# Small products of a hybrid decoder step on one Trainium2 core: samples' turns joined, transpositions and updates in one visit

## The chip, the core and the metric

The kernel runs on one core of one Trainium2 chip. TensorE does matrix products and transpositions into PSUM, VectorE and ScalarE do elementwise work and bring results out of PSUM, GpSimd does a little elementwise work and issues some stores, and SyncE issues most DMAs. The metric is the device time of one execution in microseconds. Before the change it is 835.4 us, the median of 3 runs (835.07 to 835.62).

## What is computed

One inference step of one decoder layer, for a prompt of 1024 tokens and 32 sample tokens (8 sequences of 4), model width 1024. After a conditioned RMSNorm, one wide projection feeds two branches, an mLSTM matrix memory with 4 heads in chunks of 128 tokens and a sliding-window attention with sinks (8 heads of 64, 2 key heads). Their outputs are gated, merged and projected back:

```python
h, gate = adaln_in(x, c, w_ada, b_ada, g_norm)
(mq, mk, mv, mi, mf, mo, mz, aq, ak, av, az, gm, ga) = split_in(h @ w_in)
y_m, C, n, m = mlstm_branch(mq, mk, mv, mi, mf, mo, mz, C0, n0, m0, b_i, b_f, g_mn)
...
o = sink_attend(...)
y_a = o.astype(x.dtype) * jax.nn.silu(az)
u = jax.nn.sigmoid(gm) * (y_m @ w_mo) + jax.nn.sigmoid(ga) * (y_a @ w_ao)
x = x + gate * (u @ w_o)
```

A final RMSNorm gives y. The new matrix memories, normalisers and stabilisers of prompt and samples, and the new key and value caches, are outputs too. Everything is float32.

## The kernel before

**Wide products.** A float32 product is made of three products of a faster float32 format: each operand is split into a high and a low part (hi, lo), and hi*hi, hi*lo and lo*hi are summed in PSUM. The first part of the projection runs one block of 128 columns at a time (job, job_part). From the key job of the first mLSTM head on, the columns of the projection are taken two blocks at a time, as Pair objects, and each pair is multiplied by a seven-product scheme over 2 x 2 blocks (block_products): products 1 to 7, each of 4 x 3 wide matmuls with 512 columns, into PSUM tiles bx, bw, by, bz. There are 18 pairs: four of head_in (queries, keys and values of the mLSTM heads), eight of gate, two of query_gate and four of head_gate. The order of the products is 5, 6, 2, 7, then product 1 of the next pair, then 3, 4 (for the first pair 6, 2, 7, 1 of the next, 5, 3, 4). Afterwards att_products does the same for the attention output in four AttPair objects (ax, aw, ay, az), then come mem_out and the rows of the output projection.

**The samples of a pair.** The seven-product scheme covers the 1024 prompt tokens alone. The 32 sample columns of a pair are multiplied in full float32 in Pair.samples(): 16 products with 32 output rows each (a column tile of the array), which the trace shows as 32 instructions smp (128*32). They leave four partial sums in four groups of 32 partitions of a "b" bank, which ScalarE copies to SBUF (smps). Pair.samples_end() adds the four groups by one product with a constant (smpo, two instructions in the trace, 128*128) into another "b" bank, and the kind of the pair takes the result from there. Before the change samples() of the next pair is called at the end of product 2 of a pair (product 7 for the first), and samples_end() at the end of the pair's own product 6. AttPair has the same two functions; its small products are smpa (128*32) and smpo.

**Visits.** All other work with small products (attention units, the chunks of an mLSTM head, the sample heads, the gates) is written as generators that run beside the wide products. Side.tick() is called after each k of a wide product and at the end of each product. A generator yields a lag and the names of the PSUM banks that its next step uses ("b", "o"), and tick() lets the step run when the lag is over on the kernel's own clock (side.now, line 258, an estimate in microseconds), when the banks have been left alone for HOLD (2.0 for "b", 4.0 for "o"), and, if it uses banks, when 1.5 have gone by since the last step with products (line 146). Two steps with the same bank are not run in one tick. The order of TensorE is the order of the program; VectorE and ScalarE are ordered by the framework in this stage. Each of the PSUM groups "g", "a", "b" and "o" has two banks.

**Generators that the change touches.** head(h) is one mLSTM head of the prompt: it loads, forms decays, transposes keys and values (tk, tv), and multiplies (S, U, n), in three groups of chunks (GROUPS, 3 + 3 + 2 chunks). At its end stage_c3(p) scales the rows of a group on VectorE, and stage_d(p) transposes them (ty), scales them on ScalarE and stores them. sample_head(h) does one head's samples: products stk, sS, sn, then the update of the 8 sequences' memories in three groups (sU), then the sum st and the transposition sty. The four sample heads run one after another. gates() works out the forget and input gates near the start. The "half" pool (ht) holds 49 tiles of 128 x 512 that nearly all of this work shares.

## Time and profile before

| | |
|---|---|
| median of 3 runs | 835.4 us (835.07 to 835.62) |
| the profiled execution, its own time | 835.73 us |
| its span in the profile | 833.9 us |
| TensorE busy | 813.9 us, 98% of the span |
| VectorE busy | 597.2 us, 72% |
| ScalarE busy | 421.7 us, 51% |
| mean DMA rate | 185 GB/s |
| granted TensorE clock | 0.999 |

The rows that follow in the prediction come from the profile's page, from the view of waits and from the timeline. A row of the timeline has the start (us from the span's start), the time from the first start to the last end, the engine, the line of the kernel, the operation, the tiles written and read, the array used (rows*columns), the shape of the moving operand, and the number of instructions merged into the row. The ends of matmuls overlap the starts of the next ones, so distances are taken between starts. A line can be that of a helper: L260 is mm, L265 is tr, L221 is any operation of VectorE or ScalarE. A row of waits has the waiting instruction, the one that released it, the sum, the number and the longest of the waits in us.

### The profile page before, as it was taken

What the parts mean: (1) busy time and instruction counts of PE and PEld (TensorE: products, weight loads), DVE (VectorE), ACT (ScalarE), POOL (GpSimd) and SP (SyncE); (2) the same over time, 40 slices, a digit from 0 to 9 for tenths busy, and PEclk for the clock granted to TensorE, in tenths of its full rate; (3) what the DMA queues carried; (4) which work ended last, traced back from release to release, by engine and by line L of the source; (5) the groups of instructions that cost most, each with busy time, mean ns of one, the idle gap of its engine ahead of it and who ended that gap; (6) DMA issues with size and microseconds to landing.
All of it is one profiled execution on the core that took longest, in us unless ns stands there. A gap on an engine that the chain in (4) does not pass through costs nothing. (4 is left out here: it accounts for less than half of the span.)

```text
span 833.9 us, 15075 instructions
## 1 busy us (share of the span) xinstructions
PE 813.9 (98%) x5129; PEld 665.7 (80%) x5129; DVE 597.2 (72%) x1501; ACT 421.7 (51%) x1032; POOL 67.0 (8%) x128
## 2 busy tenths in 40 slices
PE   6999999999999999999999999999999999999996
PEld 3779897888787788888888877778777779997775
DVE  4899886656656455666666776787878988874776
ACT  5664365655565564535464545344445654334343
POOL 0120000000000000000000100000002104250000
PEclk9999999999999999999999999999999999999999
DMA  9996756346445423589845433554346685643532
GB/s 342 387 362 216 197 191 203 118 155 212 140 136 162 113 102 107 172 258 309 267 146 191 134 132 113 167 178 128 128 153 205 200 287 185 205 139 127 202 108 107
DMA packets 106688, 153.95 MB, mean 185 GB/s; under 512 B 20448, under 2 KB 54368, under 8 KB 106580
## 3 DMA queue, kind: packets, MB, share of 16 engines
q1 hardware_dynamic: 100964, 142.25, 52.3%
q10 hardware_dynamic: 4176, 6.56, 2.1%
q0 software_dynamic: 1472, 4.20, 1.3%
q8 instruction: 40, 0.66, 0.3%
q14 instruction: 36, 0.29, 0.1%
HBM read 109.22 MB, written 44.75 MB: 185 GB/s over the span
## 5 line engine op out<-in xcount | busy, mean ns | idle before, releaser
L221 ACT ACTIVATE p<-p,nmx 128x256 f32<-128x256 f32 (+1 forms) x64 | 31.0, 485 | 15.6 <-DVE nmx L221 15.2
L260 PE MATMUL g_aq<-h_h,wh_aq 128*128 128x384 f32 (+1 forms) x96 | 32.3, 336 | 0.0
L221 DVE CUSTOM_DVE_ANT_0 p<-sc,cst,sink 128x256 f32<-128x256 f32 (+1 forms) x64 | 26.2, 463 | 8.3 <-PE sc L260 8.2
L260 PE MATMUL g_aq<-h_h,wl_aq 128*128 128x384 f32 (+1 forms) x96 | 30.9, 322 | 0.0
L260 PE MATMUL g_aq<-h_l,wh_aq 128*128 128x384 f32 (+1 forms) x96 | 30.8, 321 | 0.0
L260 PE MATMUL g_w_mo<-ym_l,wh_w_mo 128*128 128x384 f32 (+1 forms) x96 | 30.8, 321 | 0.0
L260 PE MATMUL g_w_mo<-ym_h,wh_w_mo 128*128 128x384 f32 (+1 forms) x96 | 30.8, 321 | 0.0
L260 PE MATMUL g_w_mo<-ym_l,wl_w_mo 128*128 128x384 f32 (+1 forms) x96 | 30.8, 321 | 0.0
L248 POOL DMA_DIRECT2D oD<-uqv x16 | 8.9, 554 | 200.0 <-ACT uqv L221 162.8
L221 ACT ACTIVATE et<-et,an 128x128 f32<-128x128 f32 x32 | 11.2, 395 | 20.7 <-DVE et L221 19.2
L260 PEld LDWEIGHTS g_aq<-h_h,wh_aq 128*128 128x128 f32 x96 | 18.0, 188 | 2.6 <-issue 1.5
L260 PE MATMUL sc<-ukv,uqv 64*128 64x256 f32 (+1 forms) x128 | 18.3, 390 | 1.3 <-DVE p L221 1.2
L221 DVE COPY p<-pt 128x512 f32<-128x512 f32 (+1 forms) x16 | 10.5, 655 | 12.0 <-PE pt L265 12.0
L260 PEld LDWEIGHTS g_w_mo<-ym_l,wh_w_mo 128*128 128x128 f32 x96 | 18.0, 188 | 0.0
L260 PEld LDWEIGHTS g_aq<-h_l,wh_aq 128*128 128x128 f32 x96 | 18.0, 188 | 0.0
L260 PEld LDWEIGHTS g_w_mo<-ym_h,wh_w_mo 128*128 128x128 f32 x96 | 18.0, 188 | 0.0
L260 PEld LDWEIGHTS g_w_mo<-ym_l,wl_w_mo 128*128 128x128 f32 x96 | 18.0, 188 | 0.0
L260 PEld LDWEIGHTS g_aq<-h_h,wl_aq 128*128 128x128 f32 x96 | 18.0, 188 | 0.0
L221 ACT ACTIVATE p<-p,den 128x256 f32<-128x256 f32 (+1 forms) x32 | 14.2, 490 | 7.4 <-DVE den L221 7.3
L221 ACT ACTIVATE sq<-rows_h 128x512 f32<-128x512 f32 (+2 forms) x14 | 8.2, 582 | 17.7 <-issue 12.0
L260 PE MATMUL g_mq<-h_h,wh_mq 128*128 128x384 f32 (+1 forms) x48 | 16.8, 350 | 0.3 <-ACT mk L221 0.3
L221 DVE TENSOR_TENSOR wor<-wor,gb 128x512 f32<-128x512 f32 x16 | 10.7, 689 | 8.7 <-DMA wor<-w_out 8.6
(2078 smaller groups left out, 2852.1 us busy)
## 6 DMA issues: line engine op xcount, KB each, us to landing
x<-xT SPq DMA_DIRECT2D x16, 256.0 KB, 5.1
early_h<-w_ada SPq DMA_DIRECT2D x8, 512.0 KB, 8.8
adar_ga<-w_ada SPq DMA_DIRECT2D x16, 256.0 KB, 4.2
wr_ga<-w SPq DMA_DIRECT2D x16, 256.0 KB, 3.4
wr_gm<-w SPq DMA_DIRECT2D x16, 256.0 KB, 3.3
taD<-gt SPq DMA_DIRECT2D x16, 256.0 KB, 2.0
tmD<-gt SPq DMA_DIRECT2D x16, 256.0 KB, 4.2
wor<-w_out SPq DMA_DIRECT2D x16, 256.0 KB, 5.3
```

Of the source, the lines that this page charges most:

```text
L221: ins = f(*args, **kw)
L248: ins = (eng or nc.sync).dma_start(out, in_)
L260: in_order(nc.tensor.matmul(out, lhsT, rhs, start=start, stop=stop, skip_group_check=more))
```

## The change

- block_products: samples_end() of a pair is no longer called behind its product 6, but directly before samples() of the next pair, behind product 2 (product 7 for the first pair). For the last pair it is called before product 3. Behind samples(), the "b" bank is marked as used and tick(True) offers a visit whether the quiet time is over or not; first_sums() comes after that visit.
- att_products: samples_end() likewise moves from behind product 6 to product 2, directly before samples() of the next pair; the last pair keeps its place.
- head(): the three scalings and the three transpositions become one step each. The third transposition goes to an "o" bank.
- sample_head(): the three updates sU run in one step, the third in an "o" bank. The scaled sum ns lies in the tile z instead of a tile of its own.
- gates(): four scratch tiles and nm, wi become parts of one tile of the "half" pool, taken at the start. The pool gets a 50th tile, and a spacer tile of 56 columns (LEAD) goes.

```diff
@@ -36,7 +36,6 @@
 
 C_ID, C_S9, C_TRI, C_CM, C_AM, C_TS, C_CS, C_RS, C_S32, C_BM, C_S64 = 0, 128, 137, 265, 393, 649, 681, 713, 745, 777, 785
 C_END = 849
-LEAD = 56
 
 
 def shape_constants():
@@ -138,12 +137,12 @@
                 if item in st["live"]:
                     st["live"].remove(item)
 
-    def tick(self):
+    def tick(self, visit=False):
         self.each()
         for st in self.streams.values():
             if st["wait"] and len(st["live"]) < st["max"] and self.now >= st["next"]:
                 self.begin(st)
-        used, visit = set(), self.now >= self.last + self.quiet
+        used, visit = set(), visit or self.now >= self.last + self.quiet
         for item in sorted((i for st in self.streams.values() for i in st["live"]), key=lambda i: i[1]):
             banks = set(item[2])
             if self.now < item[1] or used & banks or (banks and not visit) or any(self.now < self.free.get(b, 0) for b in banks):
@@ -193,7 +192,7 @@
             return ps.tile(shape, F32, tag="o", bufs=2, name=name)
 
         def ht(shape, name, dt=F32):
-            return sp.tile(shape, dt, tag="half", bufs=49, name=name)
+            return sp.tile(shape, dt, tag="half", bufs=50, name=name)
 
         def sm(shape, name, bufs=3, dt=F32):
             return sp.tile(shape, dt, tag=name, bufs=bufs, name=name)
@@ -306,7 +305,6 @@
         issue(small, a["small"])
         load_x(0, 2, KT, xT[0])
         load_x(1, 0, KT, xT[1])
-        cp.tile([128, LEAD], F32, name="lead")
         cst = cp.tile([128, C_END], F32, name="cst")
         vec = cp.tile([128, 28], F32, name="vec")
         cT, xS = (small[:, o:o + KT * n].rearrange("p (k n) -> p k n", k=KT) for o, n in ((C_TRI + 28, 9), (C_TRI + 28 + KT * 9, NS)))
@@ -598,18 +596,16 @@
         def gates(gp, zg, bias):
             gate_sums(gp, zg, (8,))
             ig = cp.tile([128, 36], F32, name="ig")
-            x = cp.tile([128, 36], F32, name="fx")
+            gt2 = ht([128, 512], "gt2")
+            x, e, r, q = (gt2[:, 256 + 36 * i:292 + 36 * i] for i in range(4))
             for t, o in ((ig, 0), (x, 4)):
                 V.memset(t, 0.0)
                 V.tensor_tensor(t[:, 0:32].rearrange("p (h c) -> p h c", c=8),
                                 gp[:, 0:8, o:o + 4].rearrange("p c h -> p h c"),
                                 bias[:, o:o + 4].unsqueeze(2).to_broadcast((128, 4, 8)), op=ALU.add)
                 V.tensor_tensor(t[:NS, 32:36], gp[:NS, 8, o:o + 4], bias[:NS, o:o + 4], op=ALU.add)
-            e = cp.tile([128, 36], F32, name="fe")
             S.activation(e, x, AF.Abs)
             S.activation(e, e, AF.Exp, scale=-1.0)
-            r = cp.tile([128, 36], F32, name="fr")
-            q = cp.tile([128, 36], F32, name="fq")
             lf = cp.tile([128, 36], F32, name="lf")
             V.tensor_scalar(r, e, 2.0, None, op0=ALU.add)
             V.reciprocal(r, r)
@@ -637,9 +633,8 @@
             tr(tp[:4, 2, 0:NS], an[:NS, 32:36], ident[:NS, :NS])
             mm(tp[:4, 3, 0:NS], lf[:NS, 32:36], cst[:NS, C_TS:C_TS + NS], start=True, stop=True)
             gt4 = ht([32, 4, 128], "gt4")
-            gt2 = ht([32, 2, 128], "gt2")
             aT, bT, zero, cm = (gt4[:, i] for i in range(4))
-            nm, wi = gt2[:, 0], gt2[:, 1]
+            nm, wi = gt2[:32, 0:128], gt2[:32, 128:256]
             aTs = cp.tile([NH, NS], F32, name="aTs")
             bTs = cp.tile([NH, NS], F32, name="bTs")
             V.tensor_copy(aT, tp[:32, 0])
@@ -1134,7 +1129,7 @@
                 m = len(cs)
                 c0, w = cs[0] * 128, m * 128
                 ns = w_.pop(p)
-                ty = pb([128, 3, 128], f"ty{h}_{p}")
+                ty = (pb, pb, po)[p]([128, 3, 128], f"ty{h}_{p}")
                 for i in range(m):
                     tr(ty[:, i], ns[:, i, 0:128], ident)
                 y = ht([128, 384], "yt")[:, :w]
@@ -1146,8 +1141,8 @@
                           [(stage_e, 1), (stage_c, 0), (stage_a, 1), 7.0, "o"],
                           [(stage_b, 1), (load, 2), 10.0, ""], [(prep, 2), 3.0, "ob"],
                           [(stage_e, 2), (stage_c, 1), (stage_a, 2), 7.0, "o"], [(stage_b, 2), 5.0, "o"],
-                          [(stage_c, 2), 5.0, ""], [(stage_f, 0), 4.0, ""], [(stage_c3, 0), 4.0, "b"],
-                          [(stage_d, 0), (stage_c3, 1), 4.0, "b"], [(stage_d, 1), (stage_c3, 2), 4.0, "b"], [(stage_d, 2), 0.0, ""]):
+                          [(stage_c, 2), 5.0, ""], [(stage_f, 0), 4.0, ""], [(stage_c3, 0), (stage_c3, 1), (stage_c3, 2), 6.0, "ob"],
+                          [(stage_d, 0), (stage_d, 1), (stage_d, 2), 0.0, ""]):
                 for fn, p in visit[:-2]:
                     fn(p)
                 yield visit[-2:]
@@ -1216,19 +1211,17 @@
             S.copy(ns4, num)
             for c, b, m in zip(Cs, bs, ns_):
                 V.tensor_tensor(c[:, :m], c[:, :m], sxb[:, h, 2, b].unsqueeze(2).to_broadcast((128, m, 129)), op=ALU.mult)
-            yield 4.0, "b"
+            yield 4.0, "ob"
             for i, (c, b, m) in enumerate(zip(Cs, bs, ns_)):
-                up = pb([128, 388], f"sU{h}_{i}")
+                up = (pb, pb, po)[i]([128, 388], f"sU{h}_{i}")
                 mm(up[:, :m * 129 + m % 2], kn, vms[i][1][:, :m * 129 + m % 2], start=True, stop=True)
                 V.tensor_tensor(c[:, :m], c[:, :m], up[:, :m * 129].rearrange("p (b e) -> p b e", e=129), op=ALU.add)
                 store(a["C_s"][h][:, b], c[:, :m, 0:128])
                 G.tensor_copy(at["n1"][:, h, b], c[:, :m, 128])
-                if i == 1:
-                    yield 1.5, "b"
             yield 3.0, "o"
             tot = po([128, 129], f"st{h}")
             mm(tot[:NS], cst[:, C_S32:C_S32 + NS], ns4, start=True, stop=True)
-            ns = sm([NS, 129], "sns", 1)
+            ns = z[:NS, 0:129]
             S.copy(ns, tot[:NS])
             ssq = sm([NS, 1], "sssq", 2)
             jk = sm([128, 128], "mjk", 2, BF16)
@@ -1524,6 +1517,8 @@
                 job_ = jobs[n]
                 nxt = jobs[n + 1] if n + 1 < len(jobs) else None
                 hook(n, i)
+                if i == 3 and not nxt:
+                    job_.samples_end()
                 job_.kind.ahead(job_, i)
                 if i == (5 if n else 6) and nxt:
                     nxt.load()
@@ -1545,7 +1540,6 @@
                         side.tick()
                 if i == 6:
                     Y = filled(pa, "by", W, n)
-                    job_.samples_end()
                 elif i == 2:
                     job_.done(0, 0, X)
                 elif i == 5:
@@ -1558,7 +1552,10 @@
                 if i == (7 if n else 5):
                     job_.done(1, 1, p5, Y)
                 if i == (2 if n else 7) and nxt:
+                    job_.samples_end()
                     nxt.samples()
+                    side.free["b"] = side.now + HOLD["b"]
+                    side.tick(True)
                     nxt.first_sums()
                 if j == 0 or (i == 3 and nxt):
                     X = NX
@@ -1742,10 +1739,12 @@
 
                 if i == 6:
                     Y = copy_of(pa, "ay", W)
-                    job_.samples_end()
+                    if not nxt:
+                        job_.samples_end()
                 elif i == 2:
                     job_.done(0, 0, X)
                     if nxt:
+                        job_.samples_end()
                         nxt.samples()
                         nxt.first_sums()
                 elif i == 5:
```

## The prediction

> **What bounds the kernel now.** I read the busy line of the page first, then TensorE's own waits, then the timeline of TensorE around the small products that the change moves.
>
> The busy line of the page:
>
> ```profile
> PE 813.9 (98%) x5129; PEld 665.7 (80%) x5129; DVE 597.2 (72%) x1501; ACT 421.7 (51%) x1032; POOL 67.0 (8%) x128
> ```
>
> Who kept TensorE waiting (us in total, times, longest):
>
> ```profile
> core 0 of [0], span 833.9 us
> ...
> PE sc L260 <- DVE p L221: 1.2, 1, 1.2
> PE bx L260 <- DVE zt L221: 0.8, 1, 0.8
> ...
> PE smpo L260 <- ACT hv L221: 0.3, 1, 0.3
> ...
> PE by L260 <- DVE hg1z L221: 0.2, 1, 0.2
> ```
>
> TensorE is busy for 98% of the span, and from the paired stage (block_products) on its waits are fractions of a microsecond to 1.2 us, none of them for a DMA. So the time of this kernel is the sum of the steps from one product's start to the next on TensorE, and an edit is worth what it takes from or adds to that chain of starts. The number of visits, work on VectorE and ScalarE, and transfers count only where one of them makes a product wait. All prices below are distances between starts. Durations are not used, because matmuls overlap.
>
> **Price of a small full-array burst.** First the timeline of TensorE around one smpo (two instructions, 128*128 array) with nothing joined to it:
>
> ```profile
> 548.20 0.33 PE L260 MATMUL smpo<-cst,smps 128*128 128x64 f32 x2
> 548.35 0.47 PE L260 MATMUL bx<-h_h,wh_pquery_gate__6438 128*128 128x512 f32 x1
> 548.66 0.40 PE L260 MATMUL bx<-h_l,wh_pquery_gate__6438 128*128 128x512 f32 x1
> 548.89 0.39 PE L260 MATMUL bx<-h_h,wl_pquery_gate__6439 128*128 128x512 f32 x1
> 549.12 0.39 PE L260 MATMUL bx<-h_h,wh_pquery_gate__6438 128*128 128x512 f32 x1
> ```
>
> A wide product (512 columns) follows the last after 0.23 us. From the burst's start to the second wide product behind it there are 548.66 - 548.20 = 0.46 us, where without the burst there would be one wide step of 0.23. The smpo burst costs 0.23 us. The first wide product behind it holds the array for 0.31 instead of 0.23, which looks like a fixed charge of 0.08 us per burst. Two bursts of transpositions show whether it is one:
>
> ```profile
> 335.00 0.49 PE L265 MATMUL ty<-cst,et 128*128 128x128 f32 x3
> 335.24 0.48 PE L260 MATMUL bx<-h_h,wh_pgate__3991 128*128 128x512 f32 x1
> 335.56 0.39 PE L260 MATMUL bx<-h_l,wh_pgate__3991 128*128 128x512 f32 x1
> ...
> 340.01 0.38 PE L265 MATMUL ty<-cst,et 128*128 128x128 f32 x2
> 340.14 0.48 PE L260 MATMUL by<-t3h,wh_pgate__4023 128*128 128x512 f32 x1
> 340.46 0.39 PE L260 MATMUL by<-t3l,wh_pgate__4023 128*128 128x512 f32 x1
> ```
>
> Three cost 0.56 - 0.23 = 0.33 us, two cost 0.45 - 0.23 = 0.22. That is 0.11 each and nothing per burst: the 0.08 behind a burst is the last product's own remainder, not a charge for changing over.
>
> **Price of a tiled burst.** The products of samples() use 32 columns of the array (128*32). One of their bursts, with the wide products around it:
>
> ```profile
> 250.48 0.40 PE L260 MATMUL bx<-h_h,wl_phead_in__3096 128*128 128x512 f32 x1
> 250.81 0.30 PE L260 MATMUL smp<-wr_mv,c 128*32 128x128 f32 x2
> ...
> 251.61 0.28 PE L260 MATMUL smp<-wr_mq,c 128*32 128x128 f32 x2
> 251.82 0.50 PE L260 MATMUL by<-t3h,wh_phead_in__3131 128*128 128x512 f32 x1
> 252.15 0.39 PE L260 MATMUL by<-t3l,wh_phead_in__3131 128*128 128x512 f32 x1
> ```
>
> Here the entry takes 0.33 (0.10 over a wide step), and the exit 0.21 with 0.33 behind it. The burst costs 1.67 - 0.46 = 1.21 us, for eight steps of four products side by side. So only a burst that leaves the full-array form has a charge at its ends, and a join can save only that.
>
> A rule of the Trainium skill goes further: the page TensorEngine Tiling (Array Packing), section Key Properties, says that changing the tiling mode, and not just the tile, drains TensorE. By that rule alone nothing is saved where full joins full, and nothing where smpo joins smp either, since the change of mode between them stays; the joins would then be worth 0 and the time would stay near 835. This page's drain agrees with the entry of 0.33 against 0.23, and the next row shows that the join is not quite worth 0.
>
> The trace has one smpo that stands directly ahead of a tiled burst (oT, 128*64, not 128*32):
>
> ```profile
> 273.25 0.39 PE L260 MATMUL bw<-t2h,wl_phead_in__3365 128*128 128x512 f32 x1
> 273.48 0.33 PE L260 MATMUL smpo<-cst,smps 128*128 128x64 f32 x2
> 273.74 0.44 PE L260 MATMUL oT<-p,ukv 128*64 128x128 f32 x4
> ```
>
> Joined, the tiled burst begins 0.23 + 0.26 = 0.49 us after the last wide product. Apart, smpo costs 0.23 and the tiled entry 0.33, together 0.56. **A join of smpo ahead of smp saves 0.07 us.** Bounds for the form that isn't shown (128*32 behind smpo): 0, if the drain is the same wherever it falls, to 0.23, if smpo vanished in it; I take 0.07, the nearest row.
>
> A visit behind the samples is shown too, here with 20 full-array products:
>
> ```profile
> 277.40 0.39 PE L260 MATMUL bx<-h_h,wl_phead_in__3408 128*128 128x512 f32 x1
> 277.72 0.30 PE L260 MATMUL smp<-wr_mk,c 128*32 128x128 f32 x2
> ...
> 280.98 0.48 PE L260 MATMUL by<-t3h,wh_phead_in__3433 128*128 128x512 f32 x1
> 281.29 0.39 PE L260 MATMUL by<-t3l,wh_phead_in__3433 128*128 128x512 f32 x1
> ```
>
> It costs 3.89 - 0.46 = 3.43; apart it would be 1.21 + 20 x 0.11 = 3.41. Such a join saves nothing.
>
> **The change, part by part.**
>
> Samples' turn: there are 18 pairs, so 17 turns in which smpo now stands ahead of smp. One of the smpo was joined to oT already and loses that. Net 16 x 0.07 = 1.1 us. The three turns of the attention pairs with a next pair (smpa, the same 128*32 form) give 0.2. The last pair's smpo moves to the step before product 3, where hook(n, i) has just issued smpa: it adds 0.15 and then 0.31 instead of 0.33 behind it, 0.13 instead of 0.23, saving 0.1. Together **-1.4**.
>
> The forced visit: samples() issues 32 products that the kernel's own clock (line 258) counts as 32 x 128/2400 = 1.7, more than the 1.5 of quiet, so the tick at the end of the same turn was already allowed to visit. Forcing it opens nothing. What is new is that visits using a "b" bank are barred there for 2.0. Full-array visits lose nothing by going alone (above). One visit to "b" behind a smp is tiled, a sample head's transposition sty:
>
> ```profile
> 506.30 0.39 PE L260 MATMUL bx<-h_h,wl_pgate__5956 128*128 128x512 f32 x1
> ...
> 507.63 0.24 PE L265 MATMUL sty<-cst,sns 32*128 32x32 f32 x1
> ```
>
> Alone it pays its own entry and exit: 0 more if it finds another tiled burst, up to 0.10 in and 0.10 out. I take **+0.2**.
>
> The forced visit also puts its VectorE work ahead of first_sums()' three additions. Between them and the first split of their result lie products 7 and 1, 24 wide steps, 5.5 us. That cover hides them; without it product 5 would wait as long as the visit's VectorE work takes.
>
> Transpositions of a head, three bursts to one, four heads: 8 bursts fewer at 0 each. Bounds 0 to 0.08 each (the remainder above), so 0 to 0.6; I take 0. The third ty takes an "o" bank, so three evacuations on ScalarE come together. Sample head's updates (sU), two bursts to one, four heads: no join of theirs is shown, bounds 0 to 0.08 each, so 0 to 0.3; I take 0, as for ty.
>
> Buffers: the "half" pool gets a 50th buffer, the gates' scratch moves into a tile of it that is held longer, samples' sums are held one product longer, ns moves into z over a column of vn whose last reader is two visits earlier. No instruction is added. The cover is that no wait of TensorE was for a load. If the pool ran dry, a load would start later and a split with it; that lies in the upper range. Addresses shift too: wide products keep the step of 0.23 in bx and by, whose operands lie in different tiles (rows above), so I price that at 0.
>
> Waits: the smpo wait of 0.3 is at a place that no longer has one, and VectorE's three small operations of the last smpo now stand behind hg1z instead of ahead of it, so the 0.2 there may go. **-0.5**. Each turn now takes both "b" banks at once. Where a visit shortly before has used them, smpo or smp waits for ScalarE's evacuation, as smpo did once for 0.3: bounds 0 to 17 times, I take one, **+0.3**. The sc and bx waits (1.2, 0.8) hang on where visits fall; they may go or have a sibling, taken at 0 with 2 us either way.
>
> Sum: -1.4 + 0.2 - 0.5 + 0.3 = -1.4 us. The profiled execution took 835.73 us (1.8 outside its span), 0.3 over the median of 835.4. From it 834.3, and against the median **834.0 us**.
>
> **Rivals.**
>
> (1) A burst does have a price: 0.08 for each that vanishes. Then the 8 ty, 4 sU and 20 smpo give 32 x 0.08 = 2.6 in place of 1.4, and if the sc wait goes as well (1.2) the time is 834.0 - 1.2 - 1.2 = 831.6, or 832.8 without it. For it: the longer wide product behind every burst. Against: two and three ty differ by exactly one product.
>
> (2) The joins are worth nothing, since the drain is paid wherever it falls: 834.0 + 1.4 = 835.4. For it: one sighting only, with another tile form. Against: that sighting.
>
> (3) Slower: both "b" banks in one turn. TensorE is in order, so a smpo that waits for its bank holds everything behind it, the next pair's products included; VectorE and ScalarE then get the pair's evacuations late. At 0.3 a turn five turns eat the gain; with 10 or more of 17 the kernel is slower by over 0.2%, and at 14 of them (13 more than the one in the sum, 3.9) it takes 837.9; I take 837.5. For it: the one smpo wait, of just this kind. Against: smp, which has its place already, does not stand among TensorE's waits for another engine, and visits to "b" are now held off behind it.
>
> **Chances.** Forecast 834.0: 0.43 (own range 833.0 to 835.2). Rival (1): 0.22. Rival (2): 0.12. Rival (3): 0.23. 0.2% (1.67 us) is about what a measurement can tell from no change. Faster by more means below 833.7: rival (1) and under half of the forecast, 0.41. Slower means above 837.1: two thirds of (3), 0.15, and 0.03 for moved waits in the other cases. The rest, 0.41, is within. The range takes rival (1) as far as its lower figure and a third of rival (3): 831.6 to 837.2, with 0.2 left out, most of it above.
>
> **What would show it.** In the changed kernel: smpo directly ahead of smp, with 0.26 between their starts and 0.33 behind (right) or over 0.30 between (rival 2). Eight ty in one burst that costs 0.88 (right) or 0.72 (rival 1). TensorE's waits: a smpo or smp wait on ScalarE in more than five turns is rival (3). I would be wrong most plainly if TensorE's total of waits moved by more than the joins did, in either direction.

## The result, and the profile after the change

The changed kernel takes 838.64 us (median of 5 runs, 837.92 to 840.19), the kernel before 835.4 us beside it. The ratio is 1.0043, with a 95% interval of 1.0031 to 1.0055. So it is slower by about 3.6 us (2.6 to 4.6 by the interval), outside the predicted range (831.6 to 837.2). Its profiled execution took 840.19 us.

The busy line and the granted clock in 40 slices, from the page of the changed kernel:

```profile
PE 815.0 (97%) x5129; PEld 670.2 (80%) x5129; DVE 595.7 (71%) x1501; ACT 420.5 (50%) x1032; POOL 69.8 (8%) x128
...
PEclk9999999999999999999899999999999999999998
```

TensorE's waits in the changed kernel (us in total, times, longest):

```profile
PE xc L259 <- ACT xsq L220: 6.2, 1, 6.2
PE S L259 <- DVE C L220: 5.9, 1, 5.9
PE pt L264 <- DVE mx L220: 1.2, 1, 1.2
...
```

The waits that the prediction quoted (sc 1.2, bx 0.8, smpo 0.3, by 0.2) are all gone by name. Where sc waited, at 287 us, pt now waits for VectorE as long (1.2), and one long wait is new: a product S of a head waits 5.9 us for VectorE's memory update C. And the twentieth slice of the clock (398 to 419 us) shows an 8.

**The joins do what they were priced at.** A joined turn of the samples and a head's joined transpositions, from the timeline of TensorE of the changed kernel:

```profile
490.99 0.39 PE L259 MATMUL bx<-h_h,wl_pgate__5730 128*128 128x512 f32 x1
491.21 0.33 PE L259 MATMUL smpo<-cst,smps 128*128 128x64 f32 x2
491.47 0.30 PE L259 MATMUL smp<-wr_ga,c 128*32 128x128 f32 x2
...
495.36 1.03 PE L264 MATMUL ty<-cst,et 128*128 128x128 f32 x8
496.15 0.48 PE L259 MATMUL bx<-h_h,wh_pgate__5800 128*128 128x512 f32 x1
496.46 0.40 PE L259 MATMUL bx<-h_l,wh_pgate__5800 128*128 128x512 f32 x1
```

smp follows smpo after 0.26, as oT did in the kernel before. Eight transpositions in one burst cost 496.46 - 495.36 - 0.23 = 0.87 us, which is 8 x 0.11 and nothing per burst.

**Where the time went.** I aligned the starts of the same wide products in two traces (by tile and count, from TensorE's first product). The table has "this kernel minus the kernel before" in us at times of the kernel before, counted from its first product, which starts 7.1 us into the span: 386 to 406 in the table is 393 to 413 in its timeline. Between 240 and 660 us the visits lie at other places, so small differences there come and go; a jump between two columns does not.

| kernel | 239 | 345 | 386 | 406 | 446 | 566 | end |
|---|---|---|---|---|---|---|---|
| changed | +1.1 | +0.7 | +2.0 | **+10.6** | +10.9 | +6.4 | +4.9 |

The front differs by 1.1 us; kernels whose front is that of the kernel before show 0.3 to 0.8 there, so most of it is the spread between executions. Between 386 and 406 us the changed kernel loses 8.6 us; over the rest of the paired stage it gains. The place in the timeline of TensorE of the changed kernel:

```profile
405.26 0.38 PE L264 MATMUL tv<-cst,hv 128*128 128x128 f32 x2
411.49 1.23 PE L259 MATMUL S<-hq,hk 128*128 128x128 f32 x4 [5.85 <-DVE C L220]
412.37 0.77 PE L259 MATMUL bw<-t2h,wh_pgate__4792 128*128 128x512 f32 x1
412.94 0.63 PE L259 MATMUL bw<-t2l,wh_pgate__4792 128*128 128x512 f32 x1
413.37 0.63 PE L259 MATMUL bw<-t2h,wl_pgate__4793 128*128 128x512 f32 x1
```

The burst (n, tk, tv and S) takes 8.67 us from its first start at 403.70 to the next wide product; without a wait it takes 2.14. That is 6.5 too many. Behind it the wide step is 0.43 instead of 0.23 for some ten steps, another 2.0. The row for 410 to 415 us below has a granted clock of 0.50.

Why C was late, from the timeline of VectorE of the changed kernel:

```profile
402.86 0.35 DVE L220 SCALAR_TENSOR_TENSOR C<-C,dec,U 128x129 f32<-128x129 f32 x1
403.13 0.69 DVE L220 TENSOR_TENSOR wl_pgate__4925<-wr_ga,wh_pgate__4924 128x512 fp32r<-128x512 f32 x1
409.99 0.56 DVE L220 TENSOR_TENSOR et<-et,cst 128x384 f32<-128x384 f32 x1 [6.18 <-DMA et<-nmd]
410.62 0.56 DVE L220 TENSOR_TENSOR qw<-qw,hq 128x384 f32<-128x384 f32 x1
411.10 0.34 DVE L220 SCALAR_TENSOR_TENSOR C<-C,dec,U 128x129 f32<-128x129 f32 x1
```

The third C needs only the product U of its own head, done since 400, and the second C. But in VectorE's order the next group's decay rows (prep: et, qw) stand ahead of it, and their load lands at 409.97. C reads the "o" bank that S, a product of another head's last group, is to write, so S waits, and TensorE with it. The load in SyncE's queue of the changed kernel:

```profile
396.76 3.19 SPq L247 DMA_DIRECT2D woDb<-wor  x3
400.89 0.32 SPq L247 DMA_DIRECT2D taD<-gt  x1
402.07 0.33 SPq L247 DMA_DIRECT2D wr_ga<-w  x1
402.46 0.42 SPq L247 DMA_DIRECT2D hq<-qD  x1
...
403.88 0.42 SPq L247 DMA_DIRECT2D et<-nmd  x1
```

The program asks for it with U, at 398.91. It is issued 5.0 us later and lands 6.1 us after its issue. Ahead of it in the queue stand three stores woDb<-wor of the output weights, which wait 3.1 us for VectorE, the store taD<-gt (0.9 for its data), the load wr_ga (0.8 for its buffer) and the head's own queries, keys and values. The same head's visit in the kernel before, on VectorE:

```profile
415.51 0.34 DVE L221 SCALAR_TENSOR_TENSOR C<-C,dec,U 128x129 f32<-128x129 f32 x1
...
418.78 0.56 DVE L221 TENSOR_TENSOR et<-et,cst 128x384 f32<-128x384 f32 x1 [1.05 <-DMA et<-nmd]
```

There C stands ahead of et, and the visit comes 9.8 us later (U at 408.72 instead of 398.91). The load itself is hardly better off: it is issued at 414.95, 6.2 us after U, and lands 10.1 us after U, where the changed kernel has 11.1. What it holds up is different: VectorE stands 1.05 us for it, with no C behind it. Windows of the kernel before and then of the changed kernel (length, busy time of PE, PEld, VectorE, ScalarE and GpSimd, granted clock, busy share of the DMA engines, GB/s):

```profile
380.00:390.00 10.00, 10.00 (x83) 8.38 (x82) 5.96 (x11) 5.23 (x19) 0.11 (x1) 1.00 1.01 302
390.00:400.00 10.00, 10.00 (x55) 8.53 (x54) 7.83 (x15) 5.12 (x12) 0.00 (x0) 1.00 0.90 305
400.00:410.00 10.00, 10.00 (x77) 8.09 (x76) 6.86 (x11) 5.44 (x13) 0.10 (x1) 1.00 0.95 287
```

```profile
390.00:395.00 5.00, 5.00 (x30) 4.32 (x28) 0.62 (x2) 1.30 (x5) 0.00 (x0) 1.00 0.83 136
395.00:400.00 5.00, 5.00 (x26) 4.25 (x26) 4.38 (x8) 1.83 (x6) 0.10 (x1) 1.00 0.96 364
...
405.00:410.00 5.00, 0.64 (x6) 0.40 (x5) 0.01 (x1) 0.00 (x0) 0.00 (x0) 0.98 0.84 194
410.00:415.00 5.00, 3.51 (x10) 3.01 (x11) 3.78 (x8) 4.38 (x16) 0.10 (x1) 0.50 0.84 307
```

In both kernels the DMA engines are nearly full here (0.83 to 1.01, and 0.63 only from 400 to 405 in the changed one). From about 406 to 410 all four compute engines stand still; only DMAs move. Much of that traffic is out_weights(), which prepares the output weights for the end of the kernel (16 loads wor<-w_out, 22 stores woD, 256 KB each).

### The profile page after: what moved, and what is told of

It reads as the page before. It is cut to its first block, busy times and chain, and to the rows that moved or that the text cites. A ratio compares the mean times of both kernels' runs of the same rounds, so it can differ in the third digit from the quotient of the medians.

```text
span 838.4 us, 15078 instructions
## 1 busy us (share of the span) xinstructions
PE 815.0 (97%) x5129; PEld 670.2 (80%) x5129; DVE 595.7 (71%) x1501; ACT 420.5 (50%) x1032; POOL 69.8 (8%) x128
## 4 chain that ended last, share of the span: by engine, by line
PE 93%; DMA 2%; DVE 2%; ACT 1%; issue 1%; SPq 1%; DVEq 0%; ACTq 0%
PE by L259 12%; PE bw L259 12%; PE bx L259 12%; PE bz L259 6%; PE g_aq L259 6%; PE g_w_mo L259 5%; PE g_mq L259 3%; PE foW L259 3%; PE foX L259 3%; PE foY L259 2%; PE smp L259 2%; PE oT L259 2%; PE foZ L259 2%; PE sc L259 2%; PE pt L264 2%; PE g_ak L259 1%
## 5 line engine op out<-in xcount | busy, mean ns | idle before, releaser
L220 DVE TENSOR_TENSOR et<-et,cst 128x384 f32<-128x384 f32 (+1 forms) x12 | 6.2, 512 | 18.1 <-DMA et<-nmd 18.1
L264 PE MATMUL pt<-cst,p 128*128 128x128 f32 x120 | 16.4, 277 | 1.2 <-DVE mx L220 1.2
```

The source lines that it names most:

```text
L220: ins = f(*args, **kw)
L264: in_order(nc.tensor.transpose(out, in_, idn))
```

## The experiments

Every ratio is against the kernel before on the same chip (medians there 835.5 to 837.2 us). Three causes stood against each other: VectorE's order, SyncE's queue, and the amount of traffic.

**Order on VectorE.** First, et and qw kept behind the earlier C of the same head; VectorE's order changes at this one place alone (w_["memory"] is the last C of the head so far).

```diff
+                early = [V.tensor_tensor(et[:, :m], ...), V.tensor_tensor(qw[:, :m], ...)]
+                for ins in early if "memory" in w_ else ():
+                    no_sync(getattr(ins, "ins", ins), [w_["memory"]])
```

> The changed kernel with one alteration of VectorE's order: the two operations of a head's prep (et, qw), which wait for a load, may not stand ahead of the head's own earlier memory updates C. Nothing else moves. Theory A (the 5.9 us wait of S is the update C that stands behind a prep whose load is late): the wait of S on C goes, no wide step of 0.43 us is left behind it, and the time falls by 5.9 + 2.0 us from the changed kernel's profiled execution, to 831.5 to 833. Rival B (S waits because the joined visits hold the o banks): S still waits for 4 us or more and the time stays at 837 to 840. Rival C (the late load blocks VectorE wherever its prep stands): the wait of S goes, but a product or bank behind VectorE waits in its place, 834 to 837.

Measured: 837.24 us, ratio 0.9992 (0.9975 to 1.0009). The waits of that kernel's TensorE:

```profile
PE smpo L259 <- ACT hv L220: 2.7, 1, 2.7
PE smp L259 <- ACT hk L220: 1.4, 1, 1.4
```

The S wait is gone, as theory A had it, but VectorE still idles 5.83 us for et (until 410.50), ScalarE stands 8.12 us behind it with et's exponentials, and the evacuations hv and hk come late for the next turn of the samples, as rival C had it. The order carries the loss against the kernel before (about 3 us of it in the traces, all of it by the medians); what the joins should have earned is still missing, because the late load finds another way.

Second, the two operations kept behind the one VectorE operation ahead of them in the program, in the changed kernel and in the kernel before:

```diff
+                    if self.name in firm and before is not None:
+                        no_sync(recent[self.name], [before])
...
+                firm.add("V")
                 V.tensor_tensor(et[:, :m], ...)
                 V.tensor_tensor(qw[:, :m], ...)
+                firm.clear()
```

> The changed kernel, and every prep keeps the place on VectorE that the program gives it, so none waits for its load ahead of work that was written before it. Theory A: VectorE's waits for et fall from 18 us to under 6, TensorE has no wait over 1.3 us in the paired stage, 830.5 to 832.5. Rival B: as the changed kernel, 837 to 840. Rival C: the same as in the kernel with only the updates put first, 834 to 837.

> The kernel before, with every prep kept in its place on VectorE in the same way. Theory A (the same hazard was there in small: the sc wait of 1.2 us lies behind a prep): VectorE's waits for et fall from 12 us to under 6, the sc wait goes, 833.5 to 834.8; so the joins of the change are worth some 2 us beside it. Rival B: no difference from before, 835.2 to 835.6.

Measured: 1.0042 (1.0027 to 1.0056) with the S wait still 6.2, since C itself was not put first (et is still ahead of it in that trace); and 0.9999 (0.9981 to 1.0017) for the kernel before. A miss for the first, no effect in the second.

**The forced visit.**

```diff
- side.free["b"] = side.now + HOLD["b"]
- side.tick(True)
```

> The changed kernel without the forced visit behind samples() and without the mark on the b bank there. Prediction's step (the forced visit opens nothing, the mark only bars b): the joins of smpo and smp stay at 0.26 us between their starts; the order of later visits shifts, so the long wait of S goes unless the same alignment comes again; 832 to 835. Rival (the forced visit itself brings the wait): it goes here and only here, with the other kernels of the change keeping it. If the wait stays, 837 to 840, the visit has no part in it.

Measured: 1.0026 (1.0014 to 1.0038), with the S wait 5.7. So the forced visit does not bring the wait.

**SyncE's queue.** et and qw issued by GpSimd, in both kernels; and, as a third, the two lines that issue the queries, keys and values moved behind et and qw.

```diff
-                    dma(t, st[d][j0:j0 + m].unsqueeze(0).to_broadcast((128, m, 128)))
+                    issue(t, st[d][j0:j0 + m].unsqueeze(0).to_broadcast((128, m, 128)), eng=nc.gpsimd)
```

> The changed kernel with one thing altered: the two small loads of a group's decay rows (et<-nmd and qw<-wid) are issued by GpSimd, at the same place of the program, so that they no longer stand in SyncE's queue behind stores that wait. Theory L (the 3 us are the price of a late load: et<-nmd, issued at 403.9 instead of 398.9 and landing at 409.97, holds VectorE, and behind it the memory update C, the o bank and TensorE): et lands before VectorE asks for it, the wait of S for C falls from 5.9 us to under 0.7, no ScalarE wait takes its place, the n/tk/tv/S turn at 404 takes 2.1 to 2.8 us instead of 8.7, no stretch at half clock, the sum of TensorE's waits falls below 5 us, and the time is 0.990 to 0.993 of the changed kernel's, that is 0.994 to 0.997 of the kernel before. Rival O (the place of C behind the decay rows in VectorE's order is the cause; or the data's way takes so long under the other traffic that an earlier issue helps little): et still comes late, S waits 3 us or more, and the time is within 0.2% of the changed kernel's.

> The kernel before with the same two loads issued by GpSimd. Theory L: its VectorE waits for et on the load go (12.0 us in 5, longest 5.0), with them the sc wait of 1.2 us and the rest of the S wait: 0.5 to 2 us faster than before (0.9976 to 0.9994), so the changed kernel with the same alteration stays 2 to 4 us ahead of it. Rival: the alteration helps both kernels alike or neither, and the changed kernel stays 3 us behind.

> The changed kernel with the order of the five loads of a group turned: et and qw first, then queries, keys, values, all still on SyncE's queue behind the same stores. Theory L: et is issued some 1.4 us earlier and lands 1.4 us earlier at the long wait (about 408.5), so the S wait is 4 to 4.9 us instead of 5.9, and the time falls by 1 to 3 us. Rival O: the wait stays within 0.5 us of 5.9.

Measured: 1.0193 (1.0173 to 1.0214), 1.0139 (1.0112 to 1.0167) and 1.0078 (1.0063 to 1.0093): what theory L forecast missed all three times, and of the rivals only the S wait within 0.5 of 5.9 in the third came. GpSimd's and VectorE's timelines in the first of them:

```profile
411.48 0.56 POOL L247 DMA_DIRECT2D et<-nmd  x1 [6.70 <-DVE gt L220]
417.21 0.55 POOL L247 DMA_DIRECT2D qw<-wid  x1 [5.17 <-DMA hk<-kD]
...
416.07 0.56 DVE L220 TENSOR_TENSOR et<-et,cst 128x384 f32<-128x384 f32 x1 [1.22 <-DMA et<-nmd]
422.04 0.56 DVE L220 TENSOR_TENSOR qw<-qw,hq 128x384 f32<-128x384 f32 x1 [5.40 <-DMA qw<-wid]
```

At this visit this trace is some 9 us late (U at 407.87). Against U, et is issued earlier, after 3.6 us instead of 5.0, and VectorE waits only 1.2 us for it. But GpSimd's queue has waits of its own: qw, the second load, stands behind another wait and is issued 9.3 us after U. VectorE idles 5.4 us for qw, with C behind it, and S waits 7.1. About 5 us more are lost at 190 to 194 us, in both kernels with this edit. And with et, qw first the S wait is 7.9 in 2, the longest 5.6: with the order turned, VectorE waits 9.4 us in 7 for the queries' load hq<-qD instead. These runs do not show that the queue is innocent, only that another queue is no way out.

**Which part brings the wait.** The joins of the heads alone, with the samples' turns as before (and the new layout):

```diff
-                if i == 3 and not nxt:
-                    job_.samples_end()
...
+                    job_.samples_end()
...
-                    job_.samples_end()
...
-                    side.free["b"] = side.now + HOLD["b"]
-                    side.tick(True)
```

> The changed kernel without its moved and joined turns of the samples: only the head's transpositions and the sample head's updates are joined, and the layout is the new one. If the long wait comes from how the moved turns shift visits against SyncE's queue, no wait of S over 1 us is left and the time is 0 to 1.5 us under that of the kernel before (0.998 to 1.000). If it comes with the joined steps of the heads (a head that ends sooner lets the next one load sooner), the wait of several us is here too and the time is above 1.002.

Measured: 1.0076 (1.006 to 1.0093), an S wait of 5.7 at the same place. The layout alone has no such wait (below), so it comes with the heads' joined steps. A head that ends sooner lets the next one begin sooner: U of this visit stands at 399.4 here, at 398.9 in the changed kernel and at 399.7 with the joins in the old layout, but at 408.7 in the kernel before and 408.9 with the layout alone. That this shift of 9 to 10 us is what turns a late load into a long wait is a reading; the shift was not made without the joins. That the kernel is 2.3 us behind the changed one at its end is more than the samples' turns are worth, and stays open.

**All readers of the late load kept back.** et and qw behind the 24 VectorE operations ahead of them in the program, and the exponentials of et behind ScalarE's 24 (the third kernel has the first half alone, the second is the kernel before):

```diff
+                past = list(V.past)
...
+                for ins in early:
+                    no_sync(getattr(ins, "ins", ins), past)
...
+                past = list(S.past)
                 for i in range(len(GROUPS[p])):
+                    ins = S.activation(et[:, i], et[:, i], AF.Exp, bias=an[:, j0 + i:j0 + i + 1])
+                    no_sync(getattr(ins, "ins", ins), past)
```

> The changed kernel with the same instructions and the same order on TensorE and in SyncE's queue; only the readers of a group's loaded decay rows are kept behind the work that stands ahead of them in the program: VectorE's two operations et and qw behind the 24 operations before them, ScalarE's exponentials of et behind the 24 before them. Theory H (head of the line: an in-order engine was given an operation whose data lands later, ahead of work that TensorE needs; the load itself need not be earlier): et<-nmd still lands about 6 us after its issue, but VectorE has other work until then, its wait for it is under 2 us, S at 404 waits under 0.7 us for C, nothing of hv or hk takes its place, the stretch from 386 to 406 us loses no more than 1 us against the kernel before instead of 8.6, and the time is 0.994 to 0.997 of the kernel before (831.5 to 834). Rival L (the load is late against what TensorE itself needs, so the wait goes to whatever reads et, as it went to hv and hk when C alone was put first): a wait of 3 us or more stays at 400 to 415 us, under another name, and the time is 1.000 to 1.004.

> The kernel before with the readers of the decay rows kept back in the same way. Theory H: it loses its sc wait of 1.2 us and some small ones and is 0 to 2 us faster than before (0.9976 to 1.000), so with the readers kept back in both, the changed kernel is 2 to 4 us the faster. Rival: what the changed kernel gains by it, the kernel before gains too, and the 3 us between them stay.

> As the one before the last, but only VectorE's two operations are kept back and ScalarE's exponentials stand where the framework puts them. If ScalarE's queue is a second head of the line, hv or hk waits of 1 to 3 us come back near 400 to 415 us and the time is 1 to 4 us above the kernel with both kept back; if VectorE alone matters, the two agree within 1 us.

Measured: 1.0023 (1.001 to 1.0037), 1.0005 (0.9993 to 1.0017), 1.0031 (1.0021 to 1.0041). What theory H forecast fell, and rival L came: a wait of the same size stays. The kernel before gains nothing. The kernels with and without ScalarE's half agree, so VectorE alone matters. VectorE of the first:

```profile
403.07 0.68 DVE L220 TENSOR_TENSOR wl_pgate__4925<-wr_ga,wh_pgate__4924 128x512 fp32r<-128x512 f32 x1
409.88 0.69 DVE L220 TENSOR_TENSOR wor<-wor,gb 128x512 f32<-128x512 f32 x1 [6.12 <-DMA wor<-w_out]
410.49 0.34 DVE L220 SCALAR_TENSOR_TENSOR C<-C,dec,U 128x129 f32<-128x129 f32 x1
```

et is out of the way, and VectorE stops at the same microsecond for **another** load, wor<-w_out, with C behind it again (S 5.8). So the stop at the head of VectorE's line is the same, and only the load it stands for has changed: whatever is loaded in this stretch is late. That pointed at the traffic itself.

**Less traffic there.** out_weights() is begun behind pair 8 or pair 6 instead of pair 5. TensorE's order does not change.

```diff
- OUT_WEIGHTS = 5
+ OUT_WEIGHTS = 8
```

> The changed kernel with one thing altered: the preparation of the output weights (out_weights: 16 loads wor<-w_out, 22 stores woDp, woDb, woDt of 256 KB each, the products on VectorE) is begun behind pair 8 instead of pair 5, some 80 us later. TensorE's order does not change. Theory D (the DMA engines are full from 376 to 414 us, so that whatever is loaded there lands 5 to 6 us after its issue; the joins bring the head's visit at 404 some 3 to 9 us nearer to its loads, and that slack is what is missing): the DMA share of 376 to 414 us falls from 0.8 to 1.0 to under 0.8, et<-nmd lands within 4 us, the S wait of 5.9 us falls under 1 us, the half clock goes, and the time is 0.993 to 0.997 of the kernel before (831 to 834). Rival O (the order on VectorE or SyncE's queue, not the amount of traffic): the S wait stays over 3 us and the time is within 0.2% of the changed kernel's, 1.002 to 1.005.

> The kernel before with the preparation of the output weights begun behind pair 8 as well. Theory D: the kernel before has few waits to lose there (S 0.4, part of sc 1.2), so it gains 0 to 2 us (0.9976 to 1.000), and with the later preparation in both the changed kernel is 2 to 4 us the faster. Rival: the kernel before gains as much as the changed one and the 3 us between them stay.

> The changed kernel with the preparation of the output weights begun behind pair 6, some 27 us later than behind pair 5. Theory D: the stretch at 404 us still has much of this traffic (the preparation takes some 75 us), but it starts at about the time when the loads of that visit are issued; the S wait falls to 0 to 4 us and the time lies between the changed kernel's and that with pair 8. Rival O: as with pair 8, no change.

Measured: changed kernel with pair 8 **832.67 us, ratio 0.9948 (0.993 to 0.9966)**; kernel before with pair 8 1.0036 (1.0019 to 1.0054); changed kernel with pair 6 1.0041 (1.002 to 1.0062). Windows of the first, and its VectorE:

```profile
380.00:390.00 10.00, 10.00 (x77) 8.34 (x76) 6.89 (x13) 5.36 (x13) 0.00 (x0) 1.00 0.48 148
390.00:400.00 10.00, 10.00 (x55) 8.55 (x54) 5.69 (x11) 5.50 (x13) 0.10 (x1) 1.00 0.48 121
400.00:410.00 10.00, 9.27 (x52) 7.77 (x51) 3.80 (x9) 5.25 (x17) 0.10 (x1) 1.00 0.52 155
```

```profile
404.44 0.56 DVE L220 TENSOR_TENSOR et<-et,cst 128x384 f32<-128x384 f32 x1 [1.39 <-DMA et<-nmd]
405.53 0.56 DVE L220 TENSOR_TENSOR qw<-qw,hq 128x384 f32<-128x384 f32 x1 [0.53 <-DMA qw<-wid]
406.01 0.34 DVE L220 SCALAR_TENSOR_TENSOR C<-C,dec,U 128x129 f32<-128x129 f32 x1
```

et still stands ahead of C, but it is issued at 399.63 instead of 403.88 and lands 4.8 us later instead of 6.1. S waits 0.7, and no half clock follows. The stores woDb<-wor are gone from SyncE's queue, and et is issued 0.7 us after U (398.94) instead of 5.0. While it is under way the DMA engines are full here too:

```profile
400.00:405.00 5.00, 5.00 (x30) 4.29 (x29) 1.70 (x4) 1.11 (x2) 0.00 (x0) 1.00 0.93 268
```

So most of what pair 8 gives this load is the earlier issue, and less is a shorter way. With the one in the old layout below, this is one of two kernels of the study that beat both: 0.9948 / 1.0043 is about 1% better than the changed kernel. The control missed: the kernel before was to gain 0 to 2 us and loses 3, so that the changed kernel is 7 us the faster with pair 8 in both, not 2 to 4. With pair 6 the DMA share from 376 to 400 is still 0.84 to 0.88 and the S wait 5.4, against the expected 0 to 4: at the head's loads the preparation is then in full swing.

**The layout.** The new layout alone (twice; the diff is this one), the changed kernel in the old layout (the same edit the other way round), and that with pair 8:

```diff
-LEAD = 56
...
-            return sp.tile(shape, dt, tag="half", bufs=49, name=name)
+            return sp.tile(shape, dt, tag="half", bufs=50, name=name)
...
-            x = cp.tile([128, 36], F32, name="fx")
+            gt2 = ht([128, 512], "gt2")
+            x, e, r, q = (gt2[:, 256 + 36 * i:292 + 36 * i] for i in range(4))
...
-            ns = sm([NS, 129], "sns", 1)
+            ns = z[:NS, 0:129]
```

> The kernel before with the changed kernel's layout alone: the 50th tile of the pool, gates() in parts of one tile, ns in z, no spacer; no turn and no visit is joined or moved. The order on TensorE is that of the kernel before. Expected by both theories: no long wait, within 1 us of the kernel before (0.999 to 1.001); if the long wait is here, the layout brings it and not the joins.

> The kernel before in the new layout alone, once more, beside the two others. Its profiled execution showed only 1.4 us of S and sc waits more than the kernel before, less than its median. If the loss is the layout's: 1.002 to 1.005 again. If it was that run's: 0.999 to 1.001.

> The changed kernel, its joins, moved turns and order on TensorE as they are, in the layout of the kernel before: 49 tiles in the pool, the spacer, gates() and ns with tiles of their own. If the layout costs what it showed alone (0.4%, 3 us), this kernel is at 0.999 to 1.001 of the kernel before, though the S wait of 5 to 6 us at 404 us is still there. If the layout costs nothing to the changed kernel, it stays at 1.003 to 1.005, with the same wait.

> The same with the preparation of the output weights begun behind pair 8. If the layout costs 3 us: 829 to 831 us, 0.990 to 0.992 of the kernel before. If it costs nothing: as with the new layout, 0.993 to 0.996.

Measured: 1.0038 (1.0023 to 1.0052) and 1.0022 (1.0009 to 1.0034) alone; 1.0038 (1.0023 to 1.0053) for the joins in the old layout; 0.9968 (0.9955 to 0.9981) with pair 8 (above both ranges that were expected). The joins in the old layout keep the S wait (4.5). So the layout does cost the kernel before 2 to 3 us, and taking it out of the changed kernel gives nothing back: the two do not add. VectorE of the layout alone:

```profile
416.64 0.56 DVE L220 TENSOR_TENSOR et<-et,cst 128x384 f32<-128x384 f32 x1 [2.85 <-DMA et<-nmd]
417.12 0.34 DVE L220 SCALAR_TENSOR_TENSOR C<-C,dec,U 128x129 f32<-128x129 f32 x1
```

Here too et has come ahead of C, and S waits 1.8 instead of 0.4. That is 1.4 of the 2 to 3 us (0.9 in the second trace, where S waits 1.3); the rest stays open.

The same wide products, aligned and timed as above:

| kernel | 239 | 345 | 386 | 406 | 446 | 566 | end |
|---|---|---|---|---|---|---|---|
| changed, C first | +1.4 | +0.4 | +1.7 | +7.9 | +8.1 | +3.6 | +2.1 |
| changed, readers kept back | +0.6 | -0.6 | +0.7 | +9.0 | +9.3 | +4.7 | +3.2 |
| heads' joins alone | +0.3 | +0.6 | +2.0 | +11.3 | +11.7 | +8.3 | +7.2 |
| changed, pair 8 | +0.7 | +0.1 | +1.4 | **+2.5** | +2.8 | -1.4 | **-2.9** |
| before, pair 8 | +0.4 | +0.4 | +1.0 | +1.0 | +2.4 | +2.7 | +2.6 |
| layout alone | +0.5 | -0.1 | +0.5 | +0.5 | +1.9 | +1.9 | +2.0 |

The jump from 386 to 406 is 8.6 in the changed kernel and 1.1 with pair 8; before and behind it the two rows run alike.

## Why the prediction was wrong

The paired stage up to the last attention product splits into 1,683 wide steps of 0.227 us (382.0 in every kernel), the small bursts (from the last wide start ahead to the second behind, less two steps) and the rest, waits between wide products above all. The bursts hold the waits inside them too:

| us | stage | bursts | rest |
|---|---|---|---|
| before | 488.4 | 100.3 | 6.0 |
| changed | 492.2 | 104.7 | 5.4 |
| changed, pair 8 | 484.9 | 98.8 | 4.0 |

- **Joins and sty, -1.2 forecast: right, at -0.9.** By that much the bursts fall when each is set at the price of the same burst without a wait, in the changed kernel and with pair 8 alike. The 0.07 of a smpo ahead of smp holds: 1.83 us joined, against 0.685 + 1.67 - 0.458 = 1.90 apart (13 of the 14 turns with nothing else in them), and the turns of the attention pairs save as much. sty costs the 0.2 it was given. Two small terms were off: st stood behind a smp once as well (0.20) and costs 0.54 alone, which the sum did not have, and the last pair's smpo saves nothing ahead of smpa (1.00 against 0.78 + 0.23), where the sum had 0.1.
- **No price per burst, rival (1): rejected**, by eight ty at 0.87. Rival (2), joins worth nothing, falls with the 0.07.
- **Waits at their bank, rival (3): not seen.** Of 17 turns one, at 336.01 us, took 2.00 instead of 1.83 without a visit joined to it. The slower side came true by another mechanism, so most of the chance that the text gave to a slower kernel stood on the wrong ground. (Rival (3)'s own sum is off too: at 0.3 a turn a loss of over 0.2% takes 12 of 17 turns, not 10.) With C put first, the late load did come out at this place, in one turn (2.7 and 1.4).
- **The forced visit, "opens nothing": read wrongly, and not what failed.** samples() calls 16 products, not 32 (the trace shows two instructions for each), so the kernel's own clock counts 0.85 for them, less than the 1.5 of quiet, and forcing can open a visit. Without it and its mark the order of TensorE is another, but the S wait stays (5.7).
- **The small waits, -0.2 forecast (-0.5 and +0.3): mis-sized.** bx went (0.8) and the sc wait got a sibling (pt, 1.2). Summed over the stage, in and between the bursts, the small waits fell by 3.9 us in the changed kernel, where the long S wait and its clock are left aside, and by 3.6 with pair 8 without its S wait.
- **The layout, "I price that at 0": not 0 by itself.** The wide step did stay, but alone the layout costs the kernel before 2 to 3 us, of which VectorE's other order shows about half; in the changed kernel taking it out gives nothing (1.0038 against 1.0043).
- **The step that failed** is the cover for the loads: "The cover is that no wait of TensorE was for a load", and, ahead of it, that transfers "count only where one of them makes a product wait". TensorE's list of waits names only the last link. VectorE's list, which was not read, had the load already:

```profile
DVE et L221 <- DMA et<-nmd: 12.0, 5, 5.0
```

and in the changed kernel:

```profile
DVE et L220 <- DMA et<-nmd: 18.1, 8, 6.2
```

Nor was the DMA line of the page of before weighed, where the 18th to 20th of the 40 slices (354 to 417 us) have 8, 9 and 8 tenths:

```profile
DMA  9996756346445423589845433554346685643532
```

The price of "a load would start later" was left in the upper range and put down to the pool running dry. It was a queue that waits and DMA engines that are full, and an order on VectorE that puts C, and so a bank of TensorE, behind the load's reader: 6.5 us at one place, and 2.0 more by the clock. The text said that it would be wrong most plainly if TensorE's waits moved by more than the joins did. They did.

Shown: the wait's path (load, VectorE, bank, TensorE), that it goes when the preparation of the output weights, with its stores in SyncE's queue and its traffic, moves away, and that it comes with the heads' joins. Not settled: how the loss divides between the late issue (4.3 us) and the slow landing (1.3 us), since pair 8 eased both; why the framework's order puts et ahead of C in some kernels and not in others; why the kernel before loses 3 us with pair 8, of which the trace shows waits of S (1.3 instead of 0.4, with et ahead of C there too) as a part; and about half of the layout's cost.

## What to carry to other kernels

An engine with no wait of its own for a transfer may still hang on one through an engine in between: read the waits of every engine that feeds it, and the DMA share of the stretch into which the change pulls work, and size the slack there before calling a load covered. A change that brings visits forward brings their loads forward, and where DMAs are full or a queue stands still the cheapest cure may be to move traffic that nobody waits for. Moving one reader aside only shows the next late load.

## What the runs showed of the hardware

- A long stop of TensorE costs more than its length. After the 5.9 us wait the clock was granted at 0.50 and the wide step was 0.43 instead of 0.23 for about 4 us behind the burst, 2.0 us in all; the kernel with C first, with stops of 2.7 and 1.4 us, had 0.75 from 415 to 420; waits of 1.8 us (layout alone) left the clock at 1.00. The Trainium skill, page TensorE: Matmul & The Clock Gate, Part 1, has the array fall to half rate after an idle window of about 3.4 us; the trace agrees with the 5.9, and that stops of 2.7 and 1.4 us close together lower it too is this run's own.
- Issuing two small loads per group from GpSimd instead of SyncE cost 1.4% in the kernel before (1.0139) and 1.5% in the changed one, though GpSimd is busy for 8% of the span. At the long wait one of the two loads was issued sooner than by SyncE (3.6 us after U instead of 5.0), and the other at 9.3: an idle engine's queue is not a free one when it has other waits in it.
